# A hybrid DeltaNet and attention layer: modulation summed on VectorE, rotary tables after it, and a wider margin for the delta rule on TensorE

## The chip, the cores and the metric

The kernel runs on one core of a Trainium2 chip. The metric is the time of one execution on the device, in microseconds, as the median of three runs. The engines' names in the profile are PE (TensorE: matmuls and transposes; PEld is its loading of weights), DVE (VectorE), ACT (ScalarE), POOL (GpSimd) and SP (SyncE, which issues every DMA of this kernel).

## What is computed

One layer over 2048 rows of 1024 numbers, all in fp32. Cut to what matters here:

```python
mod = silu(c) @ w_ada + b_ada                 # c: 1 x 1024, w_ada: 1024 x 3072
shift, scale, gate = split(mod, 3)
h = rms_norm(x, norm_g) * (1 + scale) + shift
proj = h @ w_in                               # 1024 x 4104
a_q, a_k, a_v, a_beta, a_decay, a_gate, b_q, b_k, b_v, b_gate = split(proj)
o_a = gated_delta_rule(silu(conv(a_q, a_k, a_v)), a_beta, a_decay)   # 4 heads of 128
o_b = differential_attention(rope(rms_norm(b_q)), rope(rms_norm(b_k)), b_v)   # 4 heads, 2 maps
out = x + gate * (concat(o_a * silu(a_gate), o_b * silu(b_gate)) @ w_out)
```

The rotary embedding needs tables of cosine and sine for every row. The delta rule is a recurrence over the rows: in each chunk a small triangular matrix is inverted, and a state of 128 x 128 is carried from chunk to chunk.

## The kernel before

The 2048 rows are worked in two halves of 1024, each of eight tiles of 128 rows. The projection is 18 jobs for each half, in the order of `ORDER`: `g` (gates and scalars of the delta rule), `v` and `k` (values; queries and keys of one delta head), `a` and `b` (values and gates; queries and keys of one attention head). Operands are split in a high and a low part (`hh` and `hl` of the input, both parts of a weight in one `whl` tile, or in a `wst` tile where it is read back), and three matmuls make one product. A first-half weight is loaded raw into one of two `wst` tiles, split into one of five `whl` tiles, used, and stored to DRAM (`w_d`); the second half reads it back (`w_again`). After the last job comes the attention over 16 row tiles and four heads, with the output projection (`wu`) between its pieces.

Nothing of the order is left to the hardware: a planner (`Emitter.run`) runs the kernel's parts as streams, keeps its own account of when each engine is free and each operand ready (costs in `Engine.cost`, DMA rates given to `ld`), and writes out the instruction of the stream with the smallest key next. Each engine then executes its own instructions in this order and waits at each for what it needs. The key of an instruction is the time at which its engine is free, or the time at which its operands are ready plus a margin, whichever is later; the margin is looked up in `MARGIN` by engine and by the stream's priority (0 first). An instruction that has been ready for less than its margin therefore yields to others.

```python
m = MARGIN[op.eng][min(s[0], 4)]
k = max(t, self.start(op, m) + m)
```

On PE the margins are 0 for priority 0, 100 for priority 1 and 1000 for the rest. Priority 1 holds `gdn_scalars`, `gdn_decay` and `gdn_k` with all that it calls: the transposes of `kT`, the products of chunk keys, `gdn_inverse`, `gdn_solve` (small matmuls on `mm`, `x`, `tx`, `vf`) and `gdn_scan`. The scan takes eight steps for a head and half, each of three matmuls that wait for each other through DVE or ACT: `sall,kT`, then `rr,vf`, then `vn,kd`. `gdn_out` (the outputs `o`, twice for a head and half), `gdn_v` and `gdn_q` have priority 2, the projection's own stream has 9.

The start: `mod_load` loads w_ada in eight blocks of 128 rows (1 MB each, the last in two halves) into four places, block d + 4 when block d was summed. `mod_sum` multiplies each block by its column of `sc` and adds it up on DVE in `macc`, for blocks 0 to 6. Then PE transposes `macc` (16 transposes), DVE reduces each, PE multiplies block 7 by its column (16 matmuls of one column), and DVE adds. From the sums come `acol` and `bcol`, which every element of h needs (`x_split`). Meanwhile `rotary` makes the tables (28 instructions on DVE and two on ACT), `x_load` loads the tiles of x, `x_norm` scales them, `x_transpose` transposes them on PE, and `w_load` and `w_split` bring the first weights. The table below calls the jobs by `ORDER`: g0 is the first, v0 and a1 follow. The attention needs buffers for its scores (`sr`, `sa`, `sb`); four more (`srx`) and the tiles of w_out (`wu`) are set up by `w_out_prep`, which waits until all 24 counts of the delta rule's scans and outputs are in.

## Time and profile before

| what | value |
| --- | --- |
| median of three runs | 1633.68 us (1628.46 to 1639.72) |
| the profiled execution, device time | 1633.55 us |
| its span in the profile | 1631.8 us |
| PE busy | 1514.4 us (93%) |
| DVE busy | 1200.6 us (74%) |
| ACT busy | 653.5 us (40%) |
| POOL busy | 518.1 us (32%) |
| mean granted clock of PE | 0.974 |
| DMA | 241.07 MB, 148 GB/s in the mean |

A group of instructions is named by line, engine, operation and out<-in by the program's names. Nearly every instruction is recorded by one helper, line 173, so names tell more than lines. "Idle before" is the time its engine had nothing to do just before an instruction, and the arrow tells what ended it. The granted clock of PE is 1.00 at 2.4 GHz and 0.50 at 1.2 GHz; a stretch's value is the mean.

### The profile page before, as it was taken

What the parts mean: (1) busy time and instruction counts of PE and PEld (TensorE: products, weight loads), DVE (VectorE), ACT (ScalarE), POOL (GpSimd) and SP (SyncE); (2) the same over time, 40 slices, a digit from 0 to 9 for tenths busy, and PEclk for the clock granted to TensorE, in tenths of its full rate; (3) what the DMA queues carried; (4) which work ended last, traced back from release to release, by engine and by line L of the source; (5) the groups of instructions that cost most, each with busy time, mean ns of one, the idle gap of its engine ahead of it and who ended that gap; (6) DMA issues with size and microseconds to landing.
All of it is one profiled execution on the core that took longest, in us unless ns stands there. A gap on an engine that the chain in (4) does not pass through costs nothing.

```text
span 1631.8 us, 30004 instructions
## 1 busy us (share of the span) xinstructions
PE 1514.4 (93%) x10745; PEld 1354.4 (83%) x10745; DVE 1200.6 (74%) x3215; ACT 653.5 (40%) x1589; POOL 518.1 (32%) x698
## 2 busy tenths in 40 slices
PE   2899999899999899999999999989999799999987
PEld 2888888789879888998988998967888687888866
DVE  7847868878777984777879578599799776577623
ACT  1723334232242552424234232276577555444400
POOL 0302426221330630342134133164355433234300
PEclk9999989899899899999999999989999999999999
DMA  9485543536647457252516224585424833433264
GB/s 313 144 213 146 144 141 112 157 104 177 177 84 205 146 158 243 75 172 65 160 46 200 95 88 157 163 250 176 132 81 147 240 125 116 130 111 107 75 187 148
DMA packets 226969, 241.07 MB, mean 148 GB/s; under 512 B 32540, under 2 KB 181380, under 8 KB 225924
## 3 DMA queue, kind: packets, MB, share of 16 engines
q1 hardware_dynamic: 226820, 239.16, 49.1%
q8 instruction: 84, 1.38, 0.3%
q14 instruction: 65, 0.53, 0.1%
HBM read 146.76 MB, written 92.34 MB: 147 GB/s over the span
## 4 chain that ended last, share of the span: by engine, by line
PE 67%; DVE 20%; DMA 5%; issue 3%; ACT 2%; POOL 2%; SPq 1%; DVEq 0%; ACTq 0%; POOLq 0%
PE ps L173 67%; DMA wst<-in_w_in_dram 3%; DVE srx L173 2%; DVE cv L173 2%; DVE whl L173 2%; DVE ttmp L173 1%; DVE tt L173 1%; DVE sa L173 1%; DVE sr L173 1%; DVE o L173 1%; DVE macc L173 1%; SPq L424 1%; DMA mt_o<-mix_d 1%; DVE mx L173 0%; DVE qk L173 0%
## 5 line engine op out<-in xcount | busy, mean ns | idle before, releaser
L173 PE MATMUL ps<-whl,hh 128*128 128x256 f32 (+1 forms) x2112 | 413.6, 290 | 6.2 <-DVE whl L173 5.2
L173 PEld LDWEIGHTS ps<-whl,hh 128*128 128x128 f32 x2112 | 337.3, 193 | 8.8 <-DVE whl L173 6.3
L173 PE MATMUL ps<-whl,hl 128*128 128x256 f32 (+1 forms) x1056 | 305.4, 289 | 0.0
L173 PE MATMUL ps<-hh,whl 128*128 128x512 f32 x696 | 233.9, 409 | 0.0
L173 PEld LDWEIGHTS ps<-whl,hl 128*128 128x128 f32 x1056 | 203.4, 193 | 0.1
L173 PE MATMUL ps<-kk,qt 128*128 128x512 f32 (+3 forms) x640 | 164.7, 386 | 7.1 <-DVE srx L173 2.7
L173 PE MATMUL ps<-wu,mt_s 128*128 128x512 f32 x576 | 161.0, 411 | 0.0
L173 PE MATMUL ps<-vv,pT 128*128 128x128 f32 x1088 | 152.6, 280 | 1.6 <-DVE pT L173 0.9
L173 PEld LDWEIGHTS ps<-vv,pT 128*128 128x128 f32 x1088 | 142.2, 194 | 8.7 <-ACT pT L168 1.2
L173 PEld LDWEIGHTS ps<-hh,whl 128*128 128x128 f32 x696 | 129.4, 191 | 23.9 <-issue 1.4
L173 PE MATMUL ps<-hl,whl 128*128 128x512 f32 x348 | 141.8, 407 | 0.0
L173 PEld LDWEIGHTS ps<-kk,qt 128*128 128x128 f32 x640 | 113.4, 194 | 28.0 <-DVE srx L173 4.8
L173 PEld LDWEIGHTS ps<-wu,mt_s 128*128 128x128 f32 x576 | 101.8, 189 | 17.6
L173 DVE SCALAR_TENSOR_TENSOR cv<-raw,cw,cv 128x512 f32<-128x512 f32 x144 | 111.4, 777 | 5.5 <-ACT cv L171 4.1
L168 ACT COPY pT<-ps 128x512 f32<-128x512 f32 (+3 forms) x126 | 65.9, 527 | 84.3 <-PE ps L173 81.4
L173 PE MATMUL ps<-wst,hh 128*128 128x256 f32 (+1 forms) x448 | 91.4, 291 | 0.0
L173 DVE TENSOR_SCALAR_CACHE_REDUCE sr<-ps 128x1024 f32<-128x1024 f32 (+7 forms) x88 | 74.9, 869 | 20.3 <-PE ps L173 20.0
L173 POOL TENSOR_TENSOR qrr<-qss,nhalf 128x8 f32<-128x8 f32 x32 | 54.1, 1692 | 100.6 <-DVE qss L173 99.3
L173 DVE TENSOR_TENSOR ttmp<-tt,mt 128x16 f32<-128x16 f32 (+30 forms) x248 | 81.3, 328 | 5.0
L173 PEld LDWEIGHTS ps<-hl,whl 128*128 128x128 f32 x348 | 66.6, 191 | 12.3
L173 DVE TENSOR_REDUCE tt<-ttmp 128x8 f32<-128x16 f32 (+30 forms) x248 | 72.5, 292 | 4.4
L173 POOL TENSOR_TENSOR oss<-oss,nhalf 128x1 f32<-128x1 f32 x64 | 42.2, 660 | 103.1 <-DVE oss L173 75.2
(319 smaller groups left out, 3259.0 us busy)
## 6 DMA issues: line engine op xcount, KB each, us to landing
w_d<-whl SPq DMA_DIRECT2D x52, 512.0 KB, 7.2
whl<-w_d SPq DMA_DIRECT2D x38, 512.0 KB, 4.1
mix_d<-mx SPq DMA_DIRECT2D x64, 256.0 KB, 2.6
wst<-in_w_in_dram SPq DMA_DIRECT2D x56, 256.0 KB, 6.7
mt_s<-mix_d SPq DMA_DIRECT2D x48, 256.0 KB, 3.2
xt<-in_x_dram SPq DMA_DIRECT2D x16, 512.0 KB, 4.7
q_d<-kst SPq DMA_DIRECT2D x32, 256.0 KB, 2.2
k_d<-kst SPq DMA_DIRECT2D x32, 256.0 KB, 3.2
```

What stands on the lines that cost most here:

```text
L168: call = lambda: self.nc_engine.copy(kw["out"], kw["in_"])
L173: call = lambda: getattr(self.nc_engine, fn)(**kw)
L424: return (eng or nc.sync).dma_start(out=out, in_=in_)
```

## The change

Six things are changed.

- `mod_sum`: DVE sums all eight blocks of w_ada. The sum over the partitions is made by 16 matmuls of one column, `macc` against a column of ones, into one PSUM bank, which DVE reads for `acol` and `bcol`. The transposes, the reductions and the PE part for the last block are gone.
- `rotary` begins only when the planner has written out `bcol`.
- `MARGIN` on PE is 1000 for priority 1, as for the lower priorities.
- the planner's DMA rate for w_ada and x is 360 where it was 280. The loads are the same.
- `w_again`: a weight of the second half is read back into a `wst` tile alone as long as the first half's weights are not all split, and tries `wst` before `whl` afterwards.
- one line less stands ahead of the helper: its line is 172 after the change.

```diff
-MOD_PE = 1
-MARGIN = {"PE": (0, 100, 1000, 1000, 1000), "DVE": (0, 0, 300, 300, 300), ...
+MARGIN = {"PE": (0, 1000, 1000, 1000, 1000), "DVE": (0, 0, 300, 300, 300), ...
...
-                    yield ld(big[d % 4 // 2][:, d % 2], w_ada[d * P:(d + 1) * P, 0:2 * D])
+                    yield ld(big[d % 4 // 2][:, d % 2], w_ada[d * P:(d + 1) * P, 0:2 * D], 360.0)
...
-                yield lambda: mod.get("loaded", 0) > d or d == ND - MOD_PE
-                if d == ND - MOD_PE:
-                    break
+                yield lambda: mod.get("loaded", 0) > d
...
-            red = yield small("red", 16, 1)
+            red = yield psb("mp")
             for k in (1, 0):
-                for b in range(2):
-                    pt = yield psb("mp")
-                    for i in range(4):
-                        yield TE.transpose(out=pt[:, i * P:(i + 1) * P], in_=acc[k][:, (b * 4 + i) * P:(b * 4 + i + 1) * P],
-                                           identity=ident)
-                    r = red[:, k * 8 + b * 4:k * 8 + b * 4 + 4]
-                    yield VE.tensor_reduce(out=r, in_=pt.rearrange("p (t e) -> p t e", e=P), axis=AX.X, op=ALU.add)
-                    free(pt)
-            free(*acc)
-            if MOD_PE:
-                pt = yield psb("mp")
-                for k in (1, 0):
-                    for i in range(8):
-                        for d in range(ND - MOD_PE, ND):
-                            yield TE.matmul(out=pt[:, k * 8 + i:k * 8 + i + 1],
-                                            lhsT=mod["big"][d % 4 // 2][:, d % 2, (k * 8 + i) * P:(k * 8 + i + 1) * P],
-                                            rhs=sc[:, d:d + 1], start=(d == ND - MOD_PE), stop=(d == ND - 1))
-                    r = red[:, k * 8:k * 8 + 8]
-                    yield VE.tensor_tensor(out=r, in0=pt[:, k * 8:k * 8 + 8], in1=r, op=ALU.add)
-                    if k == 1:
-                        yield from mod_scale(red)
-                free(pt)
-            else:
-                yield from mod_scale(red)
+                for i in range(8):
+                    yield TE.matmul(out=red[:, k * 8 + i:k * 8 + i + 1], lhsT=acc[k][:, i * P:(i + 1) * P], rhs=ones[:, 0:1],
+                                    start=True, stop=True)
+                if k == 1:
+                    yield from mod_scale(red)
...
         def rotary():
 
+            yield lambda: "cols" in mod
...
-                yield ld(xt, x[t * P:(t + 1) * P, :])
+                yield ld(xt, x[t * P:(t + 1) * P, :], 360.0)
...
-                t_ = yield [wp.tile([P, 1056], F32R, "whl", N_W), wp.tile([P, 1056], F32R, "wst", N_WST)]
+                al = [wp.tile([P, 1056], F32R, k, n_) for k, n_ in (("wst", N_WST), ("whl", N_W))]
+                t_ = yield al[:1 + ("ws" in mod)]
...
+            mod["ws"] = True
```

The number of instructions on the engines hardly changes, but their order does, through the whole program. Three places show how. The first is DVE's order at the start of the program, from the sum of block 5 on (`xs` and `xt` belong to the first two tiles of x, `hf` to the first x_split). Before:

```order
L173 SCALAR_TENSOR_TENSOR macc<-wa,sc,macc 128x1024 x2
L173 TENSOR_SCALAR rot<-rot 128x128 x2
L173 TENSOR_SCALAR xs<-xs 128x1
L173 SCALAR_TENSOR_TENSOR rot<-rot 128x128 x2
L173 TENSOR_SCALAR xt<-xt,xr 128x1024
L173 TENSOR_SCALAR rot<-rot 128x128
L173 TENSOR_SCALAR xs<-xs 128x1
L173 SCALAR_TENSOR_TENSOR rot<-rot 128x128
L173 TENSOR_SCALAR xt<-xt,xr 128x1024
L173 COPY cosv<-cosv 128x16x8
L173 SCALAR_TENSOR_TENSOR macc<-wa,sc,macc 128x1024 x2
L173 TENSOR_REDUCE red<-ps 128x4 x4
```

The same place now:

```order
L172 SCALAR_TENSOR_TENSOR macc<-wa,sc,macc 128x1024 x10
L172 TENSOR_SCALAR xs<-xs 128x1
L172 TENSOR_SCALAR xt<-xt,xr 128x1024
L172 TENSOR_SCALAR xs<-xs 128x1
L172 TENSOR_SCALAR xt<-xt,xr 128x1024
L172 SCALAR_TENSOR_TENSOR macc<-wa,sc,macc 128x1024 x4
L172 CAST whl<-wst 128x528
L172 TENSOR_TENSOR whl<-wst,whl 128x528
L172 TENSOR_TENSOR acol<-ps,colc 128x8
L172 TENSOR_TENSOR whl<-wst,whl 128x528
L172 SCALAR_TENSOR_TENSOR acol<-acol,colc 128x8
L172 TENSOR_TENSOR bcol<-ps,colc 128x8
```

The rotary instructions have moved behind `bcol`, among the work of job g0; the sums stand together; the cast of the first weights now stands ahead of `acol` and `bcol`. The second place is PE's order in a step of the last head's scan in the second half, from `sall,kT` to `rr,vf` (the rows between are projection matmuls). Before:

```order
L173 MATMUL ps<-sall,kT 128x128
L173 MATMUL ps<-whl,hl_6377 128x256
L173 MATMUL ps<-whl,hh_6376 128x256 x2
L173 MATMUL ps<-whl,hl_6377 128x256
L173 MATMUL ps<-whl,hh_6376 128x256 x2
L173 MATMUL ps<-whl,hl_6377 128x256
L173 MATMUL ps<-rr,vf 128x128
```

The same step now:

```order
L172 MATMUL ps<-sall,kT 128x128
L172 MATMUL ps<-whl,hl_6176 128x256
L172 MATMUL ps<-whl,hh_5860 128x256 x2
L172 MATMUL ps<-whl,hl_5861 128x256
L172 MATMUL ps<-whl,hh_5860 128x256 x2
L172 MATMUL ps<-whl,hl_5861 128x256
L172 MATMUL ps<-whl,hh_5860 128x256 x2
L172 MATMUL ps<-whl,hl_5861 128x256
L172 MATMUL ps<-whl,hh_5860 128x256 x2
L172 MATMUL ps<-whl,hl_5861 128x256
L172 MATMUL ps<-wst,hh_5860 128x256 x2
L172 MATMUL ps<-rr,vf 128x128
```

Between the two steps stand 15 projection matmuls where 7 stood; most links of most scans look like this. The third place is PE's order after the last projection matmul, among the attention's first score matmuls (`kk,qt`; a block of scores ends with `mcol,mrow`). Before, no scan step stands there:

```order
L173 MATMUL ps<-mcol,mrow 128x64
L173 MATMUL ps<-kk,qt_11903 128x256 x2
L173 LDWEIGHTS mrow
L173 MATMUL ps<-mcol,mrow 128x64
L173 MATMUL ps<-ident_r,spl 128x128 x4
L173 MATMUL ps<-kk,qt 128x384 x2
```

The same place now:

```order
L172 MATMUL ps<-mcol,mrow 128x64
L172 MATMUL ps<-sall,kT 128x128
L172 MATMUL ps<-kk,qt_11818 128x256 x2
L172 LDWEIGHTS mrow
L172 MATMUL ps<-mcol,mrow 128x64
L172 MATMUL ps<-rr,vf 128x128
L172 MATMUL ps<-ident_r,spl 128x128
L172 MATMUL ps<-vn,kd 128x128
L172 MATMUL ps<-kk,qt 128x384
```

Three steps of the last scan have moved behind the projections, and with them the two outputs of this head; before, only the transposes of the last output stood there, at the tenth block of scores. The first use of an `srx` buffer moves from the 18th block to the 27th, w_out's first matmul from the 22nd to the 30th. In the first solve of the first half (`tcp,mm`, then `x,vf`), no projection matmul stands between the two, before as after. On SP, six of the eight gate stores (`ga_d`) of the first job now stand ahead of the loads of job a1's weights, where they stood behind them. At the end of the program, 29 matmuls on `mt_s` stand between the last transpose of `ot` and the first matmul on `mt_o`, where 57 stood.

## Rows read from the trace of the kernel before

**Rows 1.** The profile's page, part 1: busy us, share of the span, instructions.

```profile
PE 1514.4 (93%) x10745; PEld 1354.4 (83%) x10745; DVE 1200.6 (74%) x3215; ACT 653.5 (40%) x1589; POOL 518.1 (32%) x698
```

**Rows 2.** Stages: length, each engine's busy us (instructions), granted clock, DMA share, GB/s.

```profile
10.00:44.00 34.00, 10.14 (x66) 9.38 (x67) 30.39 (x67) 8.54 (x15) 3.05 (x4) 0.95 1.02 328
...
93.00:600.00 507.00, 476.52 (x3599) 439.19 (x3599) 388.25 (x1041) 184.41 (x444) 159.46 (x210) 0.95 0.54 151
600.00:1058.00 458.00, 450.22 (x3510) 413.83 (x3509) 334.06 (x932) 145.88 (x370) 128.60 (x186) 1.00 0.42 133
1058.00:1100.00 42.00, 33.42 (x198) 26.49 (x196) 39.16 (x119) 31.14 (x81) 24.07 (x37) 0.88 0.78 239
...
1382.00:1570.00 188.00, 188.00 (x1136) 161.00 (x1136) 121.82 (x276) 82.15 (x180) 61.98 (x72) 1.00 0.38 113
```

**Rows 3.** Loads: stage row; SP's timeline (start, us); issues at 16.29, 19.60, 19.98 (us to landing).

```profile
20.00:26.00 6.00, 0.00 (x0) 0.00 (x0) 5.89 (x10) 3.47 (x5) 0.00 (x0) 1.00 1.02 412
...
16.29 3.64 SPq L424 DMA_DIRECT2D wa<-in_w_ada_dram  x3
...
wa<-in_w_ada_dram SPq DMA_DIRECT2D x1, 1024.0 KB, 8.9
...
wa<-in_w_ada_dram SPq DMA_DIRECT2D x1, 512.0 KB, 8.1
...
wst<-in_w_in_dram SPq DMA_DIRECT2D x1, 528.0 KB, 12.6
```

**Rows 4.** Start: groups on DVE (busy, mean ns), rotary tile's stage row, timeline (start, us).

```profile
L173 DVE SCALAR_TENSOR_TENSOR macc<-wa,sc,macc 128x1024 f32<-128x1024 f32 x12 | 14.9, 1279 | 0.0
L173 DVE TENSOR_TENSOR whl<-wst,whl 128x528 fp32r<-128x528 f32 x2 | 1.3, 705 | 0.0
...
8.00:45.00 37.00, 5.71 (x28) 0.60 (x2) 0.94 1.02 334
...
32.65 0.63 ACT L168 CAST whl<-wst 128x528 fp32r<-128x528 f32 x1 [3.28 <-DMA wst<-in_w_in_dram]
...
39.89 0.17 DVE L173 TENSOR_TENSOR bcol<-red,colc 128x8 f32<-128x8 f32 x1
...
51.16 1.86 PE L173 MATMUL ps<-ident,xt 128*128 128x128 f32 x15 [1.29 <-DVE xt L173]
```

**Rows 5.** Timeline at job a1's weights, SP and PE.

```profile
75.81 0.93 SPq L424 DMA_DIRECT2D wst<-in_w_in_dram  x2
79.97 8.59 SPq L424 DMA_DIRECT2D ga_d<-go  x6
...
92.37 0.39 PE L173 MATMUL ps<-whl,hh 128*128 128x256 f32 x1 [1.61 <-DVE whl L173]
```

**Rows 6.** PE's groups from 93 to 1058 us (last: idle before, releaser); a stage row.

```profile
L173 PE MATMUL ps<-sall,kT 128*128 128x128 f32 x128 | 26.2, 287 | 3.0 <-DVE sall L173 1.5 <-DVE sall L166 1.4
L173 PE MATMUL ps<-rr,vf 128*128 128x128 f32 x128 | 25.8, 283 | 2.0 <-DVE rr L173 2.0
...
L173 PE MATMUL ps<-vf,tx 64*64 64x64 f32 x128 | 11.6, 256 | 1.2 <-DVE tx L173 1.2
...
L173 PE MATMUL ps<-ident,kT 128*128 128x128 f32 x64 | 10.2, 276 | 2.8 <-DVE kT L173 2.8
...
L173 PE MATMUL ps<-x,vf 32*32 32x32 f32 x128 | 5.8, 197 | 2.5 <-DVE x L173 2.5
...
562.90:573.10 10.20, 7.99 (x45) 7.71 (x44) 8.86 (x19) 4.82 (x10) 8.78 (x14) 0.50 0.38 130
```

**Rows 7.** Stage rows of the instructions on o (delta outputs) and on wu (w_out) alone.

```profile
93.00:1100.00 1007.00, 17.19 (x64) 9.09 (x64) 44.93 (x96) 10.06 (x16) 0.97 0.50 146
...
1100.00:1180.00 80.00, 25.99 (x88) 15.18 (x88) 0.68 (x1) 0.00 (x0) 0.07 (x1) 1.00 0.54 164
```

**Rows 8.** PE's timeline at the end of the attention.

```profile
1556.93 13.54 PE L173 MATMUL ps<-wu,mt_s 128*128 128x512 f32 x57
1577.15 4.37 PE L173 MATMUL ps<-wu,mt_o 128*128 128x512 f32 x12 [6.67 <-DMA mt_o<-mix_d]
```

More of the change, by code (lines that the diff above doesn't have):

```diff
@@ L101 @@
 LAG = {}
-MARGIN = {"PE": (0, 100, 1000, 1000, 1000), "DVE": (0, 0, 300, 300, 300), "ACT": (0, 0, 300, 300, 300), "POOL": (0, 0, 300, 300, 300)}
+MARGIN = {"PE": (0, 1000, 1000, 1000, 1000), "DVE": (0, 0, 300, 300, 300), "ACT": (0, 0, 300, 300, 300), "POOL": (0, 0, 300, 300, 300)}
 class Op:
@@ L599, in mod_load @@
                         cs = slice(k * D, (k + 1) * D)
-                        yield ld(big[d % 4 // 2][:, d % 2, cs], w_ada[d * P:(d + 1) * P, cs])
+                        yield ld(big[d % 4 // 2][:, d % 2, cs], w_ada[d * P:(d + 1) * P, cs], 360.0)
                 mod["loaded"] = d + 1
@@ L623, in mod_sum @@
                 mod["n"] += 1
-            red = yield small("red", 16, 1)
+            red = yield psb("mp")
             for k in (1, 0):
-                for b in range(2):
-                    pt = yield psb("mp")
-                    for i in range(4):
-                        yield TE.transpose(out=pt[:, i * P:(i + 1) * P], in_=acc[k][:, (b * 4 + i) * P:(b * 4 + i + 1) * P],
-                                           identity=ident)
-                    r = red[:, k * 8 + b * 4:k * 8 + b * 4 + 4]
-                    yield VE.tensor_reduce(out=r, in_=pt.rearrange("p (t e) -> p t e", e=P), axis=AX.X, op=ALU.add)
-                    free(pt)
-            free(*acc)
-            if MOD_PE:
-                pt = yield psb("mp")
-                for k in (1, 0):
-                    for i in range(8):
-                        for d in range(ND - MOD_PE, ND):
-                            yield TE.matmul(out=pt[:, k * 8 + i:k * 8 + i + 1],
-                                            lhsT=mod["big"][d % 4 // 2][:, d % 2, (k * 8 + i) * P:(k * 8 + i + 1) * P],
-                                            rhs=sc[:, d:d + 1], start=(d == ND - MOD_PE), stop=(d == ND - 1))
-                    r = red[:, k * 8:k * 8 + 8]
-                    yield VE.tensor_tensor(out=r, in0=pt[:, k * 8:k * 8 + 8], in1=r, op=ALU.add)
-                    if k == 1:
-                        yield from mod_scale(red)
-                free(pt)
-            else:
-                yield from mod_scale(red)
+                for i in range(8):
[3 more added lines that the diff above has]
+                    yield from mod_scale(red)
             yield VE.tensor_tensor(out=bcol, in0=red[:, 0:8], in1=colc[:, 8:16], op=ALU.add)
-            free(red, *mod["big"])
+            free(red, *acc)
+            free(*mod["big"])
             mod["cols"] = True
```

## The prediction

> **What bounds the kernel now.** I read the page first: TensorE (PE) is busy for 1514.4 us, 93% of the span [rows 1]. The profiled execution took 1633.55 us in device time, the median of the three timed runs is 1633.68, so a sum made against the profile needs no shift. So what can be won is PE's idle time, 117 us of the span of 1631.8, and what a lowered clock costs.
>
> The view of stages says where they lie [rows 2]. From 10 to 44 us PE works for 10.1 us of 34 and VectorE (DVE) for 30.4: the start is DVE's. From 93 to 600 us (first half of the projections, with the delta rule between them) PE idles for 30.5 us, and its granted clock is 0.95. A granted clock is 1 or 0.5 (1.2 GHz of 2.4), so 10% of these 507 us, some 51 us, ran at half speed, which costs up to 25 us. From 600 to 1058 PE idles for 7.8 us at full clock. In the opening of the attention, 1058 to 1100, DVE is busy for 39.2 of 42 us and PE for 33.4. From 1382 to 1570 PE is busy throughout. So three places can move: the start, the delta rule in the first half, and the opening of the attention.
>
> **The change, part by part.**
>
> *The start.* Before, DVE sums seven of the eight row blocks of w_ada, with the rotary arithmetic between them; PE transposes the sums, DVE reduces them, PE does the eighth block, DVE adds. The last of it, bcol, stands at 39.89 us, and the first long stretch of PE work begins at 51.16 after a wait for DVE's xt [rows 4]. Afterwards the eight blocks are summed on DVE with no rotary work between, and 16 matmuls with a column of ones finish it.
>
> Can DVE go faster, or do the loads hold it? From 20 to 26 us the DMA engines are full, at 412 GB/s. The last three loads of w_ada are issued from 16.29 to 19.93; the last half megabyte lands 8.1 us after its issue, near 27.7 us; the projection's first weights, issued at 19.98, land 12.6 us later, at 32.6 [rows 3]. A full queue lands the same bytes at the same time even when they are asked for sooner, so I leave these two landings where they are.
>
> Now the working. Twelve accumulating passes took 14.9 us, 1.28 each [rows 4]. Blocks 6 and 7 need four, so from 25.2 (block 6 issued 16.29, landing 8.9 later [rows 3]) DVE ends them at 25.2 + 4 x 1.28 = 30.3. Its next instruction, the cast of the first weights, needs their landing at 32.6 (ScalarE's cast of the same tile starts at 32.65 after waiting for that load [rows 4]). Behind it stand, before bcol, two subtractions (1.3 us for both [rows 4]), the cast and three short operations, which I put at 1.0 together: bcol ends near 34.9 instead of 40.1. **That is 5.1 us**, and the rotary work (5.7 us of DVE busy [rows 4]) goes where DVE has room. The ones-matmuls replace as many one-column matmuls and sixteen transposes, and lie under DVE's wait for the weights. The lower bound of the gain is 0 (the next weights hold PE anyway, a rival below), the upper one 5.7 + 1.3, if the cast did not wait for its load.
>
> The Trainium skill, DMA: Bandwidth & Descriptors, "Where 436 GB/s comes from", says that loads from HBM are held by the HBM side, at about 358 GB/s. The 412 GB/s of [rows 3] lie above that, so the measurement decides; at the page's rate the 9.4 MB ahead of the first weights would land some 3.5 us later (an estimate from that page), and the start would give only about 1.5 us.
>
> *Does the gain reach the second job's weights?* Job a1's weights are issued at 75.81, when the first job's last buffers are split, and SyncE then needs 8.6 us for six gate stores; PE waits 1.61 us at 92.37 for the last of these weights [rows 5]. After the change the six gate stores stand ahead of these loads on SyncE. Their data come from the gate job, which ends 5 us earlier, so I let the loads start about 3 us earlier and the gain stand.
>
> *The delta rule's margin (100 to 1000).* The planner gives an instruction of this priority to PE only when its inputs have been ready for the margin, by its own reckoning. The order shows what follows: between a step of the scan and the next stand 15 projection matmuls where 7 stood. PE's waits at such steps, 93 to 1058 us, are 3.0 (sall,kT), 2.0 (rr,vf), 2.8 (ident,kT), 1.2 (vf,tx) and 2.5 us (x,vf), 11.5 in all [rows 6]. The x,vf wait lies where the order has no projection matmul between before or after, so it stays; of the other 9.0 I take 7. Bounds: 0 and 11.5. The clock: from 562.9 to 573.1 it stood at 0.50, PE 8.0 us busy of 10.2 [rows 6], amid such waits; its half speed cost at most 5 us, and I take 3, with 0 and 25 as bounds (all of the 51 us). **Together 10 us.** The waits of projection and output steps that kept their margin I leave as they are; their sites are drawn anew, some 5 us either way.
>
> *What is late next.* 24 links of a scan, each some 0.9 us longer, make a head's scan about 20 us longer. For seven of eight head halves the next head's work hides this. The last has nothing behind it: in the order, three scan steps and both of its output posts now stand among the attention's first score blocks, where before there was the tail of one post. Posts cost DVE 44.9 us for 16, 2.8 each [rows 7]; one and a half more are 4.2 us, in a stretch where DVE has 2.8 us of idle left in 42 [rows 2], and the scan's own steps come on top. **I take 4 us more**; below 0 it can't go, as DVE is full there, and the upper bound is the slow rival.
>
> *At no cost.* The planner's load rates (280 to 360) only set where instructions stand. The second half's weight tiles, now taken from wst first, change buffers, not bytes. At the end, 57 matmuls lay between the last ot transposes and the wait for mt_o (6.67 us [rows 8]); now 29 do. 28 of these, at 13.54/57 us each, 6.6 us, move ahead of the transposes, and the load of mt_o is queued sooner behind them: the two cancel, with 3 us either way.
>
> The sum: 1633.5 - 5.1 - 10 + 4 = 1622.4.
>
> **The rivals.**
>
> *The clock comes back.* If spreading the delta steps keeps PE dense, most of the 51 us at half clock ends: 1633.5 - 5.1 - 11.5 - 17 + 2 = 1602. For it: 600 to 1058 has the same kind of work at clock 1.00 [rows 2]. Against: only part of the low stretches lies at steps with the raised margin, and the x,vf wait stays. The Trainium skill, TensorE: Matmul & The Clock Gate, Part 1, holds that the clock follows PE's recent activity, so fewer holes would give it back; the 0.50 amid the waits at 562.9 agrees.
>
> *No change.* PE reaches a1 earlier but waits there for weights that come no sooner, behind the six stores: the start's 5 us are paid back at 92 us (its wait of 1.61 becomes 6 to 7), and the tail in the opening eats most of the margin's gain: 1633.5 - 7 + 6 = 1632.5. For it: PE already waits there [rows 5]. Against: the buffers that admit these loads come free earlier.
>
> *Slower.* The place is the attention's opening. The extra score buffers and w_out are set up only when every delta output is out. W_out's matmuls filled 26.0 us of PE between 1100 and 1180 [rows 7]. Should the late tail leave PE idle for that stretch, these 26 us are done later, where PE is full, and DVE's 9 us of posts and steps are exposed: 1633.5 - 5.1 - 7 + 35 = 1656. It decides from about 28 us of lost filler and exposed work on; against it speaks that PE idles only 8.6 us of the opening now, so most of its work there is other work.
>
> **How the numbers follow.** My forecast (1616 to 1631) has 0.46, the clock's return 0.24, no change 0.18, slower 0.12. The predicted time is the likeliest case's sum, 1622. The range, 1604 to 1640, reaches to the clock's return on one side and past no change on the other, and leaves out the slow case and the last of the fast one. About 1% (16 us) is what a measurement of this kernel can tell from no change: below 1617 lie the clock's return and a few in a hundred of the forecast, 0.31; above 1650 most of the slow case, 0.11; between them 0.58.
>
> **What would show it.** Right: bcol ending near 35 us, the long PE stretch beginning near 46; a wait at a1 of not more than 2 us; PE idle in 93 to 600 at 20 to 24 us, with waits of sall,kT and rr,vf near nothing; the opening at 42 to 46 us for the same score blocks. Wrong: a bcol at 38 or later (then the loads moved), a wait of 5 us at a1, waits at vy, o or spl grown by what sall and rr lost, or PE idle above 15 us in the attention's first 60.

## The result, and the profile after the change

The changed kernel takes 1608.3 us (median of four runs, 1604.8 to 1610.2); the ratio to the kernel before is 0.985, with a 95% interval of 0.981 to 0.989. The forecast was 1622, with a range of 1604 to 1640. So the direction and the range held; the sum behind it did not, term by term. The profiled execution has a span of 1606.8 us, 25.0 less than before.

Part 1 of the page, for the changed kernel:

```profile
PE 1504.4 (94%) x10729; PEld 1352.4 (84%) x10729; DVE 1188.3 (74%) x3218; ACT 654.5 (41%) x1583; POOL 521.7 (32%) x697
```

PE is busy for 10.0 us less [rows 1] with nearly the same instructions, and idle for 102.4 us instead of 117.4. So 10 of the 25 us are nearly the same work in less busy time, and 15 are waits.

Since the order of the whole program was written anew, the same clock times no longer hold the same work. I therefore compare at marks of equal work left: every PE instruction still to come is counted with the median time that one of its shape adds when PE works without a gap (0.119 us for 128x256, 0.111 for 128x128, 0.233 for 128x512), and a mark is where that sum passes a value. M1 (1395 us left) lies in job a1, M2 (959) near the end of the first half, M3 (523) shortly before the attention, M4 (494) after its opening, M5 (203.5) where PE has become the only limit. Two executions of one order need not agree to the tenth: again_back, below, has the changed kernel's PE order to about 330 us and stands 2.0 us later at M1, so single differences under some 2 us are not read. The table gives the time of each mark in the profiled executions, the two stretches that matter, and the measured medians.

| kernel | M1 | M2 | M3 | M4 | M5 | span | M1 to M3 | M4 to M5 | median us |
| --- | --- | --- | --- | --- | --- | --- | --- | --- | --- |
| before | 97.8 | 590.4 | 1041.3 | 1083.6 | 1410.7 | 1631.8 | 943.5 | 327.1 | 1631.4 |
| **changed** | 104.9 | 584.4 | 1029.3 | 1065.6 | 1384.2 | 1606.8 | 924.4 | 318.6 | 1608.3 |
| margin_only | 99.2 | 582.2 | 1025.2 | 1060.8 | 1387.2 | 1608.4 | 926.0 | 326.4 | 1610.1 |
| margin_back | 104.5 | 598.6 | 1051.6 | 1092.5 | 1419.5 | 1641.2 | 947.1 | 327.0 | 1646.9 |
| before_300 | 97.6 | 580.3 | 1029.4 | 1071.6 | 1394.3 | 1617.0 | 931.8 | 322.7 | 1620.2 |
| scan_only_a | 104.1 | 586.4 | 1039.4 | 1081.3 | 1412.7 | 1634.0 | 935.3 | 331.4 | 1633.7 |
| prep_only_a | 104.3 | 586.0 | 1034.6 | 1073.6 | 1398.2 | 1618.8 | 930.3 | 324.6 | 1619.9 |
| rot_early | 104.2 | 580.4 | 1025.6 | 1060.9 | 1382.4 | 1606.0 | 921.4 | 321.5 | 1608.9 |
| again_back | 106.9 | 589.8 | 1033.0 | 1068.4 | 1387.7 | 1609.3 | 926.1 | 319.3 | 1608.7 |
| rates_back | 106.6 | 591.8 | 1037.8 | 1073.1 | 1400.8 | 1621.8 | 931.2 | 327.7 | 1622.0 |
| mod_back | 104.2 | 586.1 | 1030.9 | 1067.1 | 1393.7 | 1614.6 | 926.7 | 326.6 | 1615.2 |
| rot_late | 102.9 | 579.6 | 1024.9 | 1060.3 | 1381.5 | 1603.1 | 922.0 | 321.2 | 1607.2 |
| rot_late_two | 101.8 | 582.9 | 1027.7 | 1063.3 | 1389.7 | 1613.2 | 925.9 | 326.4 | 1616.1 |

In the first two rows lies the whole result: the changed kernel is **7.1 us late** at M1, has won that back before M2, and gains 19.1 us from M1 to M3, 6.0 in the opening and 8.5 in the attention behind it; at the end 1.5 go the other way.

**The start.** Timeline of the changed kernel from 29 to 48 us, PE and then DVE (start, duration, idle before and who ended it):

```profile
29.64 3.58 PE L172 MATMUL ps<-ones,macc 128*128 128x1 f32 x16
34.57 3.57 PE L172 MATMUL ps<-ones,macc 128*128 128x1 f32 x16 [1.35 <-DVE acol L172]
...
47.34 0.79 PE L172 MATMUL ps<-whl,hh 128*128 128x264 f32 x2
...
33.26 0.44 DVE L172 CAST whl<-wst 128x528 fp32r<-128x528 f32 x1 [2.48 <-DMA wst<-in_w_in_dram]
...
38.17 0.17 DVE L172 TENSOR_TENSOR bcol<-ps,colc 128x8 f32<-128x8 f32 x1 [2.97 <-PE ps L172]
```

DVE ends its sums at 30.78 us (30.3 predicted), and its cast waits for the first weights as the prediction said (33.26). But bcol comes at 38.17: the second half of the column sums waits 1.35 us until DVE has read the first half for acol, and then needs 3.57 us. The projection's first matmul on PE stands at 47.34, where it stood at 43.84 before; but transposes that followed it before now stand ahead of it, and at equal work left PE is 1.9 us ahead of the kernel before at 70 us.

**Between 66 and 98 us.** Timeline of the changed kernel, PE, DVE, ACT and SP:

```profile
72.14 0.45 PE L172 MATMUL ps<-ident,xt 128*128 128x128 f32 x1 [2.87 <-DVE xt L172]
92.34 0.44 PE L172 MATMUL ps<-g,upi 128*128 128x32 f32 x2 [4.06 <-DVE g L172]
...
90.74 0.43 DVE L172 CAST whl<-wst 128x512 fp32r<-128x512 f32 x1 [3.32 <-DMA wst<-in_w_in_dram]
91.08 0.18 DVE L172 TENSOR_TENSOR l<-l,e 128x32 f32<-128x32 f32 x1
...
79.53 1.28 ACT L170 ACT_TABLE_LOAD   x1
82.47 1.28 ACT L170 ACT_TABLE_LOAD   x1 [1.04 <-DVE bd L172]
...
74.20 4.36 SPq L423 DMA_DIRECT2D ga_d<-go  x6
80.33 0.94 SPq L423 DMA_DIRECT2D wst<-in_w_in_dram  x2
```

PE waits for xt and for g, 6.9 us together, where before it waited 1.6 for whl [rows 5]. The chain to g stands on DVE behind a cast of a1's weights, and that cast waits for its DMA; the loads were issued 4.5 us later than before (80.33; 75.81 in [rows 5]), behind six gate stores.

Each wait costs more than its length, since the clock falls with it. The rows of two stretches of the changed kernel (length, busy us, granted clock, DMA share, GB/s):

```profile
68.00:77.00 9.00, 6.13 (x40) 5.95 (x39) 7.95 (x34) 2.71 (x7) 4.84 (x6) 0.81 0.10 34
88.00:105.00 17.00, 12.45 (x74) 10.94 (x73) 9.21 (x21) 3.50 (x8) 2.51 (x2) 0.90 0.90 229
```

By the trace's clock records it stood at 0.50 from 72.1 to 75.5 and from 92.6 to 96.0 us; before, it stood at 1.00 throughout from 66 to 98 us. At equal work left, PE's lead of 1.9 us is a lag of 2.7 after the first wait and of 8.5 after the second.

**Stages.** Length, each engine's busy us (instructions), granted clock, DMA share, GB/s. The changed kernel from M1 to M2, M2 to M3, M3 to M4 and M4 to M5, as near as whole us allow:

```profile
105.00:584.00 479.00, 453.23 (x3480) 419.44 (x3479) 364.25 (x998) 178.13 (x425) 157.77 (x211) 0.96 0.54 151
584.00:1029.00 445.00, 440.41 (x3441) 406.96 (x3440) 330.94 (x934) 146.15 (x370) 126.07 (x176) 1.00 0.41 130
1029.00:1066.00 37.00, 32.78 (x254) 29.02 (x252) 30.81 (x105) 21.88 (x59) 16.96 (x30) 1.00 0.76 234
1066.00:1384.00 318.00, 304.51 (x1998) 261.11 (x1998) 263.12 (x725) 194.17 (x491) 146.37 (x192) 0.99 0.53 161
```

The same four stretches before (the rows of [rows 2] have other bounds):

```profile
98.00:590.00 492.00, 462.23 (x3484) 425.29 (x3483) 375.67 (x1009) 175.40 (x425) 154.77 (x205) 0.95 0.54 150
590.00:1041.00 451.00, 442.61 (x3440) 405.85 (x3439) 333.00 (x923) 148.04 (x375) 129.62 (x185) 1.00 0.41 129
1041.00:1083.00 42.00, 35.09 (x239) 30.95 (x239) 32.17 (x111) 21.68 (x56) 16.75 (x30) 0.88 0.73 226
1083.00:1411.00 328.00, 307.89 (x2026) 262.76 (x2026) 264.72 (x724) 196.94 (x504) 149.45 (x194) 0.99 0.50 151
```

From M1 to M3 PE's idle time falls from 29.8 + 8.4 to 25.8 + 4.6 us, by 7.8, and its busy time from 904.8 to 893.6, by 11.2. Not all of the 11.2 is the clock's. By the clock records, half-speed time between these marks falls from 51.2 to 34.1 us, and PE's busy time in it from 45.8 to 32.5. Work that takes 13.3 us at half speed takes at least half of that at full speed, so the clock gives at most some 6.7 us; what gives the rest is not shown. In the opening the clock rises from 0.88 to 1.00 and idle time falls by 2.7. From M4 to M5 idle time falls from 20.1 to 13.5.

**Which waits.** PE's groups of the changed kernel from 93 to 1030 us (busy, mean ns; then the idle time before them and who ended it):

```profile
L172 PE MATMUL ps<-ident_r,spl 128*128 128x128 f32 x227 | 32.9, 248 | 12.2 <-DVE spl L172 8.3 <-POOL spl L172 3.8
L172 PE MATMUL ps<-sall,kT 128*128 128x128 f32 x118 | 23.3, 279 | 3.8 <-DVE sall L172 3.8
L172 PE MATMUL ps<-rr,vf 128*128 128x128 f32 x118 | 23.1, 277 | 2.2 <-DVE rr L172 1.5 <-DVE ttmp L172 0.7
L172 PE MATMUL ps<-ident,o 128*128 128x128 f32 x56 | 13.5, 274 | 0.8 <-DVE o L172 0.8
L172 PE MATMUL ps<-ident,kT 128*128 128x128 f32 x64 | 10.1, 273 | 1.9 <-DVE kT L172 1.9
L172 PE MATMUL ps<-ident,vy 128*128 128x128 f32 x64 | 10.1, 275 | 1.2 <-DVE vy L172 1.2
L172 PE MATMUL ps<-vf,tx 64*64 64x64 f32 x128 | 9.1, 221 | 0.0
L172 PE MATMUL ps<-x,vf 32*32 32x32 f32 x128 | 5.8, 198 | 6.1 <-DVE x L172 6.1
```

Before, from 93 to 1041 us, the groups that [rows 6] doesn't show:

```profile
L173 PE MATMUL ps<-ident_r,spl 128*128 128x128 f32 x224 | 32.6, 248 | 6.8 <-DVE spl L173 4.9 <-POOL spl L173 2.0
L173 PE MATMUL ps<-ident,o 128*128 128x128 f32 x56 | 15.2, 293 | 6.7 <-DVE o L173 6.7
L173 PE MATMUL ps<-ident,vy 128*128 128x128 f32 x64 | 10.3, 285 | 6.7 <-DVE vy L173 6.7
```

The sites whose margin was raised (sall, rr, kT, tx) waited 9.0 us before [rows 6] and wait 7.9 now. What is gone is the waits for o and vy (13.4 to 2.0), which had a margin of 1000 before too; what has come is waits for spl and for x (9.3 to 18.3).

### The profile page after: what moved, and what is told of

Its sections match the earlier page's. It is cut to its first block, busy times and chain, and to the rows that moved or that the text cites. A ratio compares the mean times of both kernels' runs of the same rounds, so it can differ in the third digit from the quotient of the medians.

```text
span 1606.8 us, 29971 instructions
## 1 busy us (share of the span) xinstructions
PE 1504.4 (94%) x10729; PEld 1352.4 (84%) x10729; DVE 1188.3 (74%) x3218; ACT 654.5 (41%) x1583; POOL 521.7 (32%) x697
## 4 chain that ended last, share of the span: by engine, by line
PE 66%; DVE 20%; DMA 6%; issue 3%; ACT 2%; POOL 2%; SPq 1%; DVEq 0%; ACTq 0%; POOLq 0%
PE ps L172 66%; DMA wst<-in_w_in_dram 4%; DVE ttmp L172 2%; DVE cv L172 2%; DVE whl L172 1%; DVE tt L172 1%; DVE srx L172 1%; DVE sr L172 1%; DVE sa L172 1%; DVE qk L172 1%; SPq L423 1%; DVE oss L172 1%; DVE sb L172 1%; DVE macc L172 1%; DVE o L172 0%
## 5 line engine op out<-in xcount | busy, mean ns | idle before, releaser
L172 PE MATMUL ps<-whl,hh 128*128 128x256 f32 (+1 forms) x2080 | 405.6, 290 | 0.5 <-DVE whl L172 0.5
L172 PEld LDWEIGHTS ps<-whl,hh 128*128 128x128 f32 x2080 | 330.1, 192 | 2.2 <-DVE whl L172 0.9
L172 PE MATMUL ps<-whl,hl 128*128 128x256 f32 (+1 forms) x1040 | 301.2, 290 | 0.0
L172 PE MATMUL ps<-hh,whl 128*128 128x512 f32 x688 | 227.1, 405 | 0.0
L172 PEld LDWEIGHTS ps<-whl,hl 128*128 128x128 f32 x1040 | 199.1, 191 | 0.4
L172 PE MATMUL ps<-kk,qt 128*128 128x512 f32 (+3 forms) x640 | 159.5, 380 | 4.8 <-DVE sb L172 2.6
L172 DVE TENSOR_SCALAR_CACHE_REDUCE sr<-ps 128x1024 f32<-128x1024 f32 (+7 forms) x98 | 82.9, 872 | 25.6 <-PE ps L172 25.6
L172 PE MATMUL ps<-wst,hh 128*128 128x256 f32 (+1 forms) x480 | 96.7, 292 | 0.5 <-ACT hf L170 0.5
L172 PEld LDWEIGHTS ps<-wst,hh 128*128 128x128 f32 x480 | 76.4, 193 | 1.5 <-ACT hf L170 0.7
```

The costliest lines, as they stand in the source:

```text
L172: call = lambda: getattr(self.nc_engine, fn)(**kw)
```

## The experiments

Each was timed against the kernel before on the same chip, in five rounds; the ratios are to it, with 95% intervals. The kernels are the changed one with one thing altered, unless the name or the text says before.

### The margin alone, and all but the margin

margin_only is the kernel before with the one number; margin_back is the changed kernel without it.

```diff
-MARGIN = {"PE": (0, 100, 1000, 1000, 1000), ...
+MARGIN = {"PE": (0, 1000, 1000, 1000, 1000), ...
```

> The kernel before with one number changed: PE's margin of priority 1 is 1000. Theory A, read from the two traces (the changed start is a loss, the margin gives more than the whole gain): the start is that of before, bcol near 40 us, PE waits of 1.6 us at job a1's weights; from 93 us on the margin gives what the changed kernel gave after 220 us, 25 + 8 = 33 us: about 1600 us. Theory B, that of the prediction (start 5 us, margin 10, tail 4 back): about 1627 us. Theory C (the 13 us that the changed kernel wins between 1180 and 1410 us, inside the attention, depend on how the whole order falls out and not on the margin): about 1613 us.

> The changed kernel with PE's margin of priority 1 back at 100; all else as changed. Theory A (the start loses): the 8 us lost by 105 us stay lost and nothing is won behind them, about 1640 us. Theory B (the start wins 5 us): about 1628 us. Theory C (the order's chances): within 10 us of 1630, with another distribution of waits in the attention.

margin_only took 1610.1 us (0.986, 0.983 to 0.989), margin_back 1646.9 (1.010, 1.007 to 1.013; its profiled execution, with a span of 1641.2, is one of its shortest). The margin is worth 22 us by itself and 39 in the changed kernel; everything else in the change costs 15 us with the old margin and, within what was measured, nothing with the new one. Theory B, the prediction's, falls on both. Theory A's direction holds: the start package loses 6.7 us at M1 and margin_only 1.4. But margin_only doesn't reach 1600, since it has the attention of before (326.4 us from M4 to M5, against 318.6 of the changed kernel), as theory C said. Stage rows of margin_only, M1 to M2 and M2 to M3:

```profile
99.00:582.00 483.00, 455.77 (x3487) 420.80 (x3486) 370.64 (x1008) 179.86 (x431) 155.86 (x208) 0.96 0.54 153
582.00:1025.00 443.00, 439.49 (x3439) 406.36 (x3438) 329.45 (x930) 144.11 (x366) 124.33 (x176) 1.00 0.42 132
```

Idle 30.7 and busy 895.3 us: nearly the figures of the changed kernel (30.4 and 893.6). So the gain from M1 to M3 is the margin's: over all orders run here this stretch takes from 921.4 to 931.2 us with 1000 for the whole of priority 1, and 943.5 and 947.1 with 100. Its opening (M3 to M4, 35.6 us) is also that of the changed kernel. Three of its PE groups, from 93 to 1025 us:

```profile
L173 PE MATMUL ps<-sall,kT 128*128 128x128 f32 x118 | 23.9, 285 | 7.5 <-DVE sall L173 4.6 <-DVE sall L166 2.9
L173 PE MATMUL ps<-ident,o 128*128 128x128 f32 x56 | 13.8, 285 | 0.8 <-DVE o L173 0.8
L173 PE MATMUL ps<-ident,vy 128*128 128x128 f32 x64 | 10.1, 275 | 1.4 <-DVE vy L173 1.4
```

With the one number changed, the waits for o and vy fall from 13.4 to 2.2 us, and the wait for sall, at the scan's own link, grows from 3.0 to 7.5. In margin_back, with the old margin, o and vy wait 11.0 us.

### Which instructions the margin acts on

scan_only_a gives 1000 to the scan's matmuls alone, prep_only_a to all priority-1 instructions but these. The line is put into the planner, here for scan_only_a; prep_only_a has the two numbers the other way round.

```diff
                         m = MARGIN[op.eng][min(s[0], 4)]
+                        if s[0] == 1 and op.eng == "PE":
+                            m = 1000 if any(a.tensor.name.split("_")[0] in ("sall", "rr", "vn") for a in op.ins) else 100
```

> The changed kernel with the margin of 1000 on PE only for the matmuls of the scan (those that read sall, rr or vn); all other priority-1 instructions have 100. Against the changed kernel (1608 us) and the same with 100 everywhere (1647). Theory P, that of the prediction (the gain lies where the links of a scan wait for each other): most of the 39 us is kept, 1610 to 1618 us. Theory Q (it lies in what a head does ahead of its scan: the transposes of kT, the products of keys, the inverse and the solve): 1635 to 1647 us.

> The changed kernel with the margin of 1000 on PE for all priority-1 instructions but those of the scan, which have 100. Theory P (the scan's links): 1635 to 1647 us. Theory Q (what stands ahead of the scan): 1610 to 1618 us. If this and the run with the scan alone both keep half, the gain is spread over both kinds, 1622 to 1632 us each.

scan_only_a took 1633.7 us (1.001, 0.999 to 1.003), prep_only_a 1619.9 (0.993, 0.990 to 0.995). Against 1646.9 with neither, the scan is worth 13 us, what stands ahead of it 27, and in these medians the two add up to the 39 of both. By the marks, from M1 to M3 alone, they are worth 11.8 and 16.8, and both together 22.7: there they do not add up, and part of the medians lies behind M3, in the order that each kernel drew. So the larger part lies where theory Q put it, in the transposes, products, inverse and solve, but the scan's links have their share. Stage rows, M1 to M2 and M2 to M3, of margin_back, scan_only_a and prep_only_a:

```profile
104.00:599.00 495.00, 462.51 (x3497) 425.19 (x3496) 378.68 (x1020) 177.96 (x428) 154.10 (x204) 0.95 0.52 146
599.00:1052.00 453.00, 445.29 (x3438) 409.08 (x3437) 331.02 (x921) 145.41 (x371) 126.07 (x182) 0.99 0.40 127
```

```profile
104.00:586.00 482.00, 456.42 (x3484) 419.88 (x3483) 376.01 (x1020) 176.19 (x423) 145.64 (x199) 0.96 0.53 148
586.00:1039.00 453.00, 448.50 (x3438) 412.89 (x3437) 329.01 (x929) 143.25 (x368) 124.91 (x178) 0.98 0.41 129
```

```profile
104.00:586.00 482.00, 455.32 (x3489) 421.19 (x3489) 371.49 (x1008) 180.19 (x429) 151.94 (x205) 0.96 0.54 151
586.00:1035.00 449.00, 442.56 (x3442) 407.15 (x3442) 328.42 (x918) 146.88 (x374) 131.90 (x189) 1.00 0.41 128
```

With neither, PE idles for 40.2 us and is busy for 907.8. The scan alone takes 10.1 us of idle time away and 2.9 of busy time; what stands ahead of it takes 7.1 and 9.9. The clock came back with the second, not with the first: the half-speed time from M1 to M3 is 54.6 us with neither, 54.6 with the scan alone and 37.5 with what stands ahead of it.

### How large a margin

before_300 is the kernel before with 300 in place of 100; margin_3000 is the changed kernel with 3000.

```diff
+MARGIN = {"PE": (0, 300, 1000, 1000, 1000), ...        (before_300)
+MARGIN = {"PE": (0, 3000, 1000, 1000, 1000), ...       (margin_3000)
```

> The kernel before with PE's margin of priority 1 at 300 in place of 100 (with 1000 it took 1610 us, with 100 it takes 1632). Theory G (the margin covers inputs that come some 100 to 300 ns later than the planner reckons): 300 gives most of the gain, 1608 to 1616 us. Theory H (what counts is that the delta rule has the same margin as the other streams, so that it no longer goes ahead of the outputs o, the values vy and the projection): little of the gain, 1625 to 1635 us.

> The changed kernel with a margin of 3000 for priority 1 on PE instead of 1000 (100: 1647 us; 1000: 1608). Theory W (a larger reserve keeps spreading the delta rule's instructions, but what is left of idle time at the scans is at links with no other work between): from the place of 105 us to that of 1030 us within 4 us of the changed kernel, with the last head's outputs later still (block 20 of scores instead of 8); the opening of the attention 2 to 6 us longer. Theory X (the stretch of the attention, 319 to 332 us in the runs so far, depends on the order that the planner happens to write): 319 to 332 us, whatever the margin. In all 1603 to 1620 us. Rival Y (the gain grows with the margin): under 1600 us.

before_300 took 1620.2 us (0.993, 0.990 to 0.996): half of what 1000 gives, between theories G and H, so neither is the whole story. From M1 to M3 it has 931.8 us, 11.7 less than before. margin_3000 took 1676.9 us (1.028, 1.024 to 1.032) and all three theories missed it: it loses 34 us against before between M1 and M3 alone. In its order part of the computation comes out changed, and which part is not known, so nothing else is made of its time. In before_300 the waits for o and vy are already down to 2.1 us, at half of the gain.

### What loses the start

Four runs undo one thing each. rot_early drops the wait ahead of the tables, rot_late makes it longer (until the delta rule's scalars of the first half), rates_back drops the rate of 360, mod_back takes `mod_sum` and `rotary` from the kernel before; again_back restores the old rule for weight buffers.

```diff
-            yield lambda: "cols" in mod                       (rot_early, mod_back)
...
-            yield lambda: "cols" in mod                       (rot_late)
+            yield lambda: ctx_half[0].get("scal")
...
-                yield ld(xt, x[t * P:(t + 1) * P, :], 360.0)  (rates_back, w_ada's loads likewise)
+                yield ld(xt, x[t * P:(t + 1) * P, :])
...
-                t_ = yield al[:1 + ("ws" in mod)]             (again_back)
+                t_ = yield [wp.tile([P, 1056], F32R, "whl", N_W), wp.tile([P, 1056], F32R, "wst", N_WST)]
```

> The changed kernel with the rotary tables made from the start on, as before, between the sums of w_ada. Theory A (the tables' 5.9 us of DVE work and their neighbours at 66 to 80 us make xt late by 2.9 us and feed the wait for g of 4.1 us): bcol 2 to 4 us later, near 41 us, but no wait at xt near 70 us, and at equal remaining work near 105 us it is 3 to 6 us ahead of the changed kernel; in all about 1603 us. Theory D (the wait for g comes from the weights of job a1 behind six gate stores, the tables do nothing): as late at 105 us as the changed kernel or 2 us later, about 1610 us.

> The changed kernel with the old rule for the second half's weight buffers (whl first, then wst, at any time). PE's order is the same for its first 2960 instructions, to about 330 us. By the prediction (this edit costs and gives nothing): 1608 us, with 5 us either way for the order behind. Rival: the edit kept the first half's split from waiting for a whl tile; then the waits of PE on whl between 330 and 600 us come back (3.7 us before, 0.5 after) and it takes 1613 to 1618 us.

> The changed kernel with the planner's rate for the loads of w_ada and x back at 280. Theory E (the rate is what loses the start: at 360 the planner takes x for landed too soon and puts the transposes of tiles 8 and 9 some 21 to 30 projection matmuls ahead of where they stood; PE waits 2.9 us for xt at 69 us, its clock falls, DVE's split of job v0's weights and with it the loads of a1's weights come 4.5 us late, and PE waits 4.1 us for g): no wait for xt of over 1 us near 70 us, the first loads of a1's weights issued near 76 us, and at the same remaining work PE stands near 97 us where the changed kernel stood at 105. In all 1600 us if that is kept, 1605 if the attention takes half of it back. Rival F (the loss comes from the sums or the tables, the rate has no part): still at 103 to 105 us there, 1608 us.

> The changed kernel with the rotary tables still later: they begin when the delta rule's scalars of the first half are done (after neg), not at bcol. Theory R (the start is lost to the tables: 5.9 us of DVE work and two loads of ACT's function tables, 1.28 us each, stand among the gates of job g0 from 66 to 84 us and make xt, the split of v0's weights and g late): no wait for xt of over 1 us near 70 us, no wait for g, and at the same remaining work PE stands near 97 us where the changed kernel stood at 105; in all about 1600 us if that is kept, 1605 if the attention takes half of it back. Theory S (the loads of a1's weights are late because six gate stores stand ahead of them on SyncE): the wait for g becomes one of 4 us or more for whl, 103 to 106 us at that place, 1608 us.

> The changed kernel with the modulation and the rotary tables of before (seven blocks on DVE, the eighth on PE, the tables between the sums); margin 1000, rates of 360 and the new rule for weight buffers stay. Theory R (the sums and tables as changed lose the start): bcol near 40 us, the tables done before 45 us, and at the same remaining work PE stands near 98 us where the changed kernel stood at 105; 1600 to 1610 us. Rival T (rates and buffer rule lose it, in whatever way the sums are made): 104 to 106 us there.

rot_early took 1608.9 us (0.986, 0.983 to 0.989), again_back 1608.7 (0.986, 0.983 to 0.989), rates_back 1622.0 (0.994, 0.992 to 0.996), rot_late 1607.2 (0.983, 0.981 to 0.985), mod_back 1615.2 (0.988, 0.986 to 0.991). At M1 all five stand at 102.9 to 106.9 us, 5 to 9 later than before. No single edit is the cause: with the old sums and tables (mod_back) the loss is there, and with the old rates (rates_back) it is there; margin_only, which has none of these edits, loses 1.4 us. rates_back shows besides that the planner's rates, which move no byte, are worth 14 us of order: 7 from M1 to M3 and 9 from M4 to M5. again_back bears the prediction out: that edit is worth nothing that was measured.

What the five have in common is the place. rot_late, PE and then SP, from 71 to 96 us:

```profile
90.74 0.39 PE L172 MATMUL ps<-whl,hh 128*128 128x256 f32 x1 [0.46 <-DVE whl L172]
93.37 0.38 PE L172 MATMUL ps<-whl,hh 128*128 128x256 f32 x1 [1.78 <-DVE whl L172]
95.83 0.58 PE L172 MATMUL ps<-whl,hh 128*128 128x256 f32 x1 [2.08 <-DVE whl L172]
...
71.94 3.89 SPq L423 DMA_DIRECT2D ga_d<-go  x6
76.47 0.94 SPq L423 DMA_DIRECT2D wst<-in_w_in_dram  x2
79.72 1.00 SPq L423 DMA_DIRECT2D wst<-in_w_in_dram  x2
```

The waits for xt and g are gone, as theory R wanted; in their place are 4.3 us for whl, as theory S said. In mod_back the same place, PE and then SP:

```profile
87.14 0.41 PE L173 MATMUL ps<-g,upi 128*128 128x32 f32 x2 [3.27 <-DVE g L173]
97.42 0.39 PE L173 MATMUL ps<-whl,hh 128*128 128x256 f32 x1 [2.87 <-DVE whl L173]
...
75.14 0.93 SPq L424 DMA_DIRECT2D wst<-in_w_in_dram  x2
```

Here the loads are issued earlier than before, bcol stands at 36.47, PE was 4.5 us ahead of before until 70 us, and it waits all the same. Six stores ahead of the loads can therefore not be what the five share: here the first four loads of a1's weights stand ahead of the stores, and the last of them lands at 90.54 us, 91.81 before. That the loss arises at this place is shown; what holds it there in every one of these orders is open. rot_late_two asks the question from the other side: it takes rot_late and gives the two halves of the column sums a PSUM bank each, so the start gets shorter and nothing else is meant to change.

```diff
             red = yield psb("mp")
+            red2 = yield psb("mp")
...
-                    yield TE.matmul(out=red[:, k * 8 + i:k * 8 + i + 1], ...
+                    yield TE.matmul(out=(red if k else red2)[:, k * 8 + i:k * 8 + i + 1], ...
```

> The kernel with the tables after the scalars, and the two halves of the modulation's column sums in two PSUM banks, so that PE's second sixteen one-column matmuls no longer wait until DVE has read acol from the first bank (a wait of 3.4 us there, 1.4 in the changed kernel). Theory U (the start is held at 90 to 105 us by the weights of job a1, whose loads wait for buffers; what is won before that is paid back there): bcol 1.5 to 3.5 us earlier, 35 to 37 us, the work before 80 us as much earlier, but PE at the place of 105 us within 2 us of the kernel with one bank (+5 to the kernel before); 1605 to 1609 us, or the draw of the attention's order decides. Rival V (the start counts in full): 2 to 3 us ahead there, 1604 us.

In DVE's timeline of this kernel bcol comes 2.4 us sooner than in rot_late (38.64):

```profile
36.23 0.17 DVE L172 TENSOR_TENSOR bcol<-ps,colc 128x8 f32<-128x8 f32 x1 [1.43 <-PE ps L172]
```

At M1 1.1 of the 2.4 us are left, which two executions can differ by. So theory U is not contradicted, and V's "2 to 3 us ahead" is not seen; U is borne out better by mod_back, where 4.5 us of lead are gone and 6.4 lost at M1. In time it took 1616.1 us (0.991, 0.987 to 0.995), 9 us more than rot_late, and not because of the start: 3.9 are lost from M1 to M3 and 5.2 from M4 to M5, by another order.

### The attention's order

No run was made for it alone. In PE's order as the traces have it (buffer numbers left out), the part from the first score matmul on is the same in its last 3212 of 3260 instructions for before and margin_back, in 3272 of 3288 for margin_only and rates_back, and in all 3288 for rot_early and rot_late. These pairs take 327.1 and 327.0, 326.4 and 327.7, and 321.5 and 321.2 us from M4 to M5, although they arrive at M4 up to 12 us apart. The other orders take from 318.6 (the changed kernel) to 331.4. So this stretch's time belongs to the order that the planner happened to write, and the same waits come back with it. PE's groups from 1060 to 1420 us, before and in margin_back:

```profile
L173 PE MATMUL ps<-ident,sr 128*128 128x128 f32 x147 | 24.5, 280 | 5.8 <-DVE sr L173 2.9 <-ACT oj L171 1.5 <-DVE mx L173 1.2
```

```profile
L172 PE MATMUL ps<-ident,sr 128*128 128x128 f32 x143 | 24.1, 282 | 5.9 <-DVE sr L172 3.3 <-DVE mx L172 1.3 <-ACT oj L170 1.2
```

The changed kernel's order happens to be the best of them, with again_back's (319.3) close to it: its row has 3.5 us. No kernel run here beats it by more than its measurement is uncertain.

## Why the prediction was right and wrong

| term | predicted | measured, by the marks |
| --- | --- | --- |
| start, to M1 | -5.1 | +7.1 |
| margin, M1 to M3 | -10 (7 idle, 3 clock) | -19.1 (7.8 idle, 11.2 busy) |
| opening, M3 to M4 | +4 | -6.0 |
| attention, M4 to M5 | 0 | -8.5 |
| end | 0, 3 either way | +1.5 |
| sum | -11 | -25.0 |

The first four terms miss by 8 to 12 us each, one upward and three downward. That their sum stays inside the range, 18 us either way, is in part luck.

**The start.** Right were the loads (block 6 landed at 25.24, the first weights at 33.23 us), the sums on DVE and the cast that waits behind them. Two steps failed. That the ones-matmuls "lie under DVE's wait for the weights" held for the first sixteen only: the second sixteen stand behind DVE's reading of acol, and DVE waits 2.97 us for them, so bcol came at 38.17, not 34.9. The prediction had a bcol at 38 or later as a sign that the loads had moved; they had not. Of the 5.1 us, 1.9 were there at 70 us. And "I let the loads start about 3 us earlier and the gain stand" was the wrong choice between two cases the prediction had itself: its rival put the start's gain as lost at a1's weights, behind the six stores. The gain was gone behind the wait for xt at 72 us, and by the wait at a1's weights 7.1 us on top of it, part of that by the clock, which fell in both waits. That the stores are the cause is not shown (mod_back). The rotary work did not go "where DVE has room" either: it stood among the gates at 66 to 82 us. But its place is not the cause by itself, since neither rot_early nor rot_late gives the loss back.

**The rates** stood under "At no cost". That step failed: rates_back shows 14 us. A number that only sets where instructions stand is not free where the order decides the waits.

**The margin.** The total of idle time won was right (7.8 us for 7), its sites were not: the links that the prediction priced wait nearly as before (9.0 and 7.9 us), while the waits for o and vy, which it left "as they are", went from 13.4 to 2.0, and those for spl and x grew by 9.0. That the margin does this to o and vy is shown: they wait 13.4 and 11.0 us in the two kernels with 100 for the delta rule, and 2.0 and 2.2 in the changed kernel and margin_only. Why is not shown; that equal margins make the streams take turns can't be all of it, since 300 against their 1000 does the same (2.1 us in before_300). The mis-sized term was the clock: 3 us taken, while busy time fell by 11.2, of which the clock gave at most some 6.7. In the clock records, the half-speed time of the whole execution fell from 88.0 to 62.2 us. The Trainium skill, TensorE: Matmul & The Clock Gate, Part 1, has the clock follow PE's recent activity; the falls at 72.1 and 92.6 us, each at the end of a wait of PE, agree. The sum of idle time does not tell the clock: prep_only_a, which removes less idle time than scan_only_a (7.1 against 10.1 us), loses 17.1 us of half-speed time, scan_only_a none.

**The opening.** The late tail of the last scan did move there, but its price has the other sign: 42.3 us became 36.3. M3 lies 17 and 13 us ahead of the first score matmul; counted from that matmul, the 19th block of scores ends at 41.4 us where it ended at 42.7, the 22nd at 46.4 instead of 53.4. The row of the first 42 us of scores in the changed kernel, and the stretch from M3 to M4 in scan_only_a:

```profile
1042.80:1084.80 42.00, 35.61 (x252) 29.57 (x251) 39.19 (x130) 29.67 (x83) 20.05 (x34) 1.00 0.78 237
```

```profile
1039.00:1081.00 42.00, 35.40 (x249) 31.05 (x248) 28.67 (x98) 20.95 (x58) 18.24 (x34) 0.88 0.61 193
```

DVE is as full as the prediction said (39.19 of 42 us, 39.16 before [rows 2]). The step that failed is that the added work must then make PE wait: from M3 to M4 its idle time fell from 6.9 to 4.2 us, and the clock stayed at 1.00 where it had been 0.88. Why is open. It is not enough that the scan's steps give PE work between the scores, since scan_only_a has such steps there too and takes 41.9 us at 0.88. The slow rival's mechanism never showed.

**The attention** had no term, and 8.5 us lie there. The prediction took it for granted that a stretch whose work isn't changed keeps its time; its order was changed.

**The end** came within its bound: the wait for mt_o is 5.52 us, 6.67 before [rows 8].

**The rivals.** The result lies between the forecast's own range (from 1616) and the clock's return (1602), and has something of the second: the clock did come back, in part. "No change" named the place of the start's loss and the length of PE's waits (6 to 7 us; 6.9 measured, though for xt and g), but not that the start would lose 7.1 us beyond its gain. What came, faster by over 1%, had a chance of 0.31; the forecast left out more of the clock than it took, and the attention's order.

## What to carry to other kernels

Where a planner writes the order, an edit to its numbers redraws all waits: price it by what orders of this kind have cost (here some 13 us between the best and the worst attention for the same work), not only by the waits that it is meant for, and compare two traces at equal work left. A gain ahead of a place where loads hold the engine can be lost there (the 4.5 us of mod_back), so look for the next wait on weights before counting a start. A reserve for one stream also moves the waits of the streams beside it, whose numbers nobody touched: look at theirs as well as its own. And less busy time is not all clock: read the clock records beside it.

## What the runs showed of the hardware that was not expected

The granted clock reads 1.00 in stage rows that lie ahead of its first record (33.8 us before, 48.2 in the changed kernel), while the durations say half speed: fifteen transposes of xt take 3.46 us at 26 and 30 us and 1.86 at 51 us [rows 4]; sixteen one-column matmuls take 3.57 us at 34.57 in the changed kernel and 1.95 at 35.50 before, where PE had transposed and multiplied since 28.5. So the shorter work on PE at the start was also slower work.

The loads of ACT's function tables cost 1.28 us each, at 79.53 and 82.47 us for the one switch to the sine and back. The Trainium skill, ScalarE: Activation LUTs, "What ACT_TABLE_LOAD costs", adds a drain of some 1.4 us to every switch; here the next activation starts 1.30 us after the load's start (80.83), so no drain shows, and the trace's time is the one that counts.

Loads of 256 KB of weights that are issued at 79 to 84 us land some 13 us later (79.20 to 91.81 before, 83.97 to 96.79 in the changed kernel). In these stretches (76 to 92 and 80 to 97 us) the DMA engines move 148 and 142 GB/s at a busy share of 0.79 and 0.76, where w_ada's loads moved 412 at 1.02 [rows 3]: they are busy for twice as long per byte. What in these transfers makes them slow no run here tells apart.
